# A decoder trunk on Trainium2: the classical sum of up leaves its bank earlier, p2 is multiplied second, and a layer's first feed-forward block has classical pairs only

## The chip, the cores and the metric

The kernel runs on one core of a Trainium2 chip, as one program with one launch. Its time is the device time in microseconds; the median of three runs counts. A core has TensorE (matrix products, into the banks of PSUM), VectorE and ScalarE (elementwise work, both read PSUM), GpSimd, and SyncE, which issues most DMA transfers from HBM. Each engine works through its own list of instructions in order and waits on semaphores of the others.

## The reference, cut to what matters

256 tokens of width 2048 pass through two layers. Each has a token-mixing part (differential attention, a gated recurrence, gated linear attention) and then the feed-forward part, where the change lies:

```python
for l in range(DEPTH):                       # 2 layers
    h = rms_norm(x, pre_mix_norm[l])
    ...                                      # 12 + 4 blocks of products, mixers
    h = rms_norm(x, pre_ffn_norm[l])
    hid = silu(einsum('bsd,df->bsf', h, w_ffn_gate[l])) * einsum('bsd,df->bsf', h, w_ffn_up[l])
    ff = einsum('bsf,fd->bsd', hid, w_ffn_down[l])
    x = x + rms_norm(ff, post_ffn_norm[l])
```

All is float32; the width of hid is 5632 = 11 x 512.

## The kernel before, in words

**Products.** An operand is kept as two float32r parts, hi + lo. Each product of 128 x 128 activations by 128 x 512 weights is three matmuls into one PSUM accumulator of 128 x 512 (hi.hi, hi.lo, lo.hi; `multiply`, L433, matmuls at L437 to L439; in `block`, L402 to L404). 256 tokens are two halves, t = 0 and 1. Weights come by DMA in pieces of 512 KB (two chunks of 128 x 512, tile `raw`, five buffers). `split` (L337) makes the parts of a chunk: ScalarE casts hi (tile `hilo`, ten buffers), VectorE subtracts to get lo. `feed` (L366) runs splits ahead of the products, at most ten of them, for a split needs a `hilo` buffer that an earlier product has left. All ScalarE and VectorE instructions are issued at L180, a helper, so they are told apart by their tiles.

**The feed-forward part.** hid is made in 11 blocks of 512 columns, f = 0 to 10, gate and up together (`gate_up`, `pair_block`, L442). The products with the down weights stand between them, as `ffn_order` (L56) says: after f = 0 none, after f = 1 to 8 two blocks, after f = 9 four, after f = 10 the last four. A down block has four chunks for each f that its part holds: part 0 is f = 0 alone, so the four down blocks after f = 1 and f = 2 have four chunks each; most others have eight.

**C and S pairs.** A block takes the 16 chunks of the contraction two at a time, eight pairs. A C pair is classical: 2 matrices x 2 chunks x 2 halves = 8 products, 24 matmuls. An S pair gets the same with seven products, 21 matmuls, by a Strassen-like scheme. It multiplies sums of weight chunks (t1 to t4, made by VectorE, then split like the rest) and sums of activations (the "forms", made once per layer by `make_forms`). The order of pairs is "CSCSCSCS", for f = 1 "CCSCSCSS". The classical sums and some of the seven products share accumulators: x (up, second half of the tokens), p2, q4 and q3 lie in the four banks of tag `acc`, as do the two accumulators of each down block; p1, q5 and p6 with p7 lie in others (tags `tr`, `o`, `sc`). In the profile gu_p stands for p1, p2, p6 and p7, and gu_q for q3, q4 and q5.

**Working a block off.** `evac` is called after each product of the last S pair, in the order of PRODUCTS (L104). ScalarE copies p1 to m1; VectorE then makes, with eight additions, u2 and u3 (tile u) and c11, c12, c21, c22 (tiles c_c). x is read by one of these: c22 + x, after q4. A job, `hidden`, later applies silu and the product with up, turns the rows with TensorE (tile tpu) and splits them into hid.

**The first block.** f = 0 starts while the normalised activations are still arriving, chunk by chunk. Its order is 12 single chunks of gate, six of up, an S pair, six of up, an S pair (FIRST_ORDER, L53): two S pairs. `make_forms` is called in one go after the 12 chunks of gate: one addition of 128 x 2048, four of 128 x 512, and four splits, in the queues of VectorE and ScalarE at that place.

**Order.** The order of instructions is the program's. Side work (norms, `hidden`, scales) is written as jobs that a small planner (`Lane`) runs between products, by a clock that it estimates itself; `lane.require` runs jobs until something is done.

Of the kernel before, what the change touches and what calls it, by code (L numbers as in the profile page):

```python
# [19 lines left out]
P = 128  # L20
S = 256
# [26 lines left out]

# [3 lines left out]
FIRST_C = 6  # L52
FIRST_ORDER = "G" * 2 * FIRST_C + "UUUUUUSUUUUUUS"  # L53

# [13 lines left out]
def pair_order(f):  # L68


    order = []
    if f == 0:
        at = {"G": 0, "U": 0, "S": FIRST_C}
        for kind in FIRST_ORDER:
            order += quad(at[kind]) if kind == "S" else [("GU".index(kind), at[kind])]
            at[kind] += 1
        return order
    at = {"C": 0, "S": N_C}
    for kind in SECOND_PAIRS if f == 1 else PAIRS:
        p = at[kind]  # L80
        at[kind] += 1
        order += quad(p) if kind == "S" else [(m, k) for m in range(2) for k in (2 * p, 2 * p + 1)]
    return order
# [19 lines left out]
QUAD = ("b11", "t1", "t2", "t3", "t4", "b21", "b22")  # L103
PRODUCTS = ("p1", "q5", "p6", "p7", "q4", "p2", "q3")  # L104
# [95 lines left out]
def tile_hybrid_trunk(ctx, tc, x, xT, w_in, w_out, w_gu, w_down, post_norms, lams,  # L200
# [74 lines left out]
    for l in range(DEPTH):  # L275
        for n0, n in IN_ORDER:
            plain(w_in[l][:, n0:n0 + n], DC)
        cols = [slice(b * 512, (b + 1) * 512) for b in range(4)]
        for c in cols:
            plain(w_out[l][:, c], DC)  # L280
        for kind, f, b in ffn_order():
            if kind == "down":
                f0, f1 = FFN_PARTS[f]
                plain(w_down[l][f0 * 512:f1 * 512, cols[b]], 4 * (f1 - f0))
                continue
            recipes, i = [], 0
            for kind in FIRST_ORDER if f == 0 else SECOND_PAIRS if f == 1 else PAIRS:
                k = 1 if kind in "GU" else 4
                recipes += [(name, i) for name in QUAD] if kind == "S" else [("raw", i + j) for j in range(k)]
                i += k  # L290
            add_block([w_gu[l, f, i] for i in range(DC)], recipes)
# [3 lines left out]
    for b, (n, count) in enumerate(blocks):  # L295
        b %= per_layer
        w = b in (0, 14, 15, 16, per_layer - 2, per_layer - 1) and len(wider) > 0
        wider += [w and i % 8 in (1, 4, 6) and (b != 16 or i < 2 * FIRST_C) for i in range(count)]

    read_by, left = [], Counter()  # L300
    for b, kind, i in items:
        for c in {"raw": (i,), "b11": (i + 1,), "t2": (i,), "b21": (i + 2,), "b22": (i + 3,)}.get(kind, ()):
            left[c // 2] += 1
    full_at = 0
    for b, kind, i in items:
        for c in {"raw": (i,), "b11": (i + 1,), "t2": (i,), "b21": (i + 2,), "b22": (i + 3,)}.get(kind, ()):
            left[c // 2] -= 1
        while full_at in left and left[full_at] == 0:
            full_at += 1
        read_by.append(full_at)  # L310
# [26 lines left out]
    def split():  # L337
# [7 lines left out]
        if kind == "b11":  # L345
            up1, gate1, up2 = raw_chunk(i), raw_chunk(i + 1), raw_chunk(i + 3)
            dve.free = max(dve.free, raws[(i + 3) // 2][1])
            summed("t1", gate1, up1)
            summed("t2", sums["t1"], up2)
# [7 lines left out]
        if kind == "t2":  # L357
            summed("t3", raw_chunk(i), raw_chunk(i + 3))
            summed("t4", sums["t2"], raw_chunk(i + 2))
# [82 lines left out]
    def pair_block(f, ah, al, forms, hidden_before, evac):  # L442
# [11 lines left out]
        acc = {k: pp.tile([P, 512], F32, tag="acc", name=f"gu_{k}", bufs=4) for k in ("x", "q4", "p2", "q3")}  # L454
# [11 lines left out]
        last_c = 2 * (FIRST_C if f == 0 else N_C)  # L466

        def classic(j, m, c, t):
            k = sums_of[m][t]
            n_c[k] += 1  # L470
            multiply(acc[k], parted(c, t), j, begin(k), k == "x" and n_c[k] == last_c)
            lane.tick()

        def seven(j, p, final):
            if "p1" not in acc:
                lane.require(*hidden_before)
                acc["p1"] = pp.tile([P, 512], F32, tag="tr", name="gu_p1", bufs=1)
                acc["q5"] = pp.tile([P, 512], F32, tag="o", name="gu_q5", bufs=1)
                sc = pp.tile([P, 2, 512], F32, tag="sc", name="gu_p67", bufs=1)
                acc["p6"], acc["p7"] = sc[:, 0, :], sc[:, 1, :]  # L480
# [14 lines left out]
        if f == 0:  # L495
            at = [0, 0]
            while min(at) < last_c:
                able = [t for t in range(NT) if at[t] < last_c and (t == 1 or at[0] - at[1] < AHEAD)
                        and done.get(("h", t, at[t]), math.inf) <= lane.clk]
                if not able:  # L500
                    lane.idle()
                    continue
                t = min(able, key=lambda t: at[t])
                feed(j + at[t] + 1)
                classic(j + at[t], 0, at[t], t)
                at[t] += 1
                used[0] = j + min(at)
                if ("h", 1, 7) not in done:
                    feed(j + at[0] + LOOK_F, used[0])
                else:  # L510
                    feed(used[0] + LOOK_W, used[0])
            j += last_c
            forms.extend(make_forms(ah, al))
            at = {"U": 0, "S": FIRST_C - N_C}
            for kind in FIRST_ORDER[last_c:]:
                p = at[kind]
                at[kind] += 1
                if kind == "S":
                    seven(j, p, p == N_S - 1)
                    j += 7  # L520
                    continue
                feed(j + 1)
                for t in range(NT):
                    classic(j, 1, p, t)
                j += 1
                used[0] = j
                feed(j + LOOK_W, j)
            return
# [229 lines left out]
    for l in range(DEPTH):  # L758
# [530 lines left out]
        def make_forms(ah, al):  # L1289

            full = mw[:, 0, :].rearrange("p (c t) -> p c t", t=S)[:, :2 * N_S, :]
            lane.require(*(("h", 1, c) for c in range(DC)))
            dve.tensor_tensor(out=full, in0=ah[:, 2 * N_C:, :].bitcast(F32), in1=al[:, 2 * N_C:, :].bitcast(F32),
                              op=ALU.add)
# [3 lines left out]
            dve.tensor_tensor(out=s1, in0=a21, in1=a22, op=ALU.subtract)  # L1298
            dve.tensor_tensor(out=s3, in0=a11, in1=a21, op=ALU.subtract)
            dve.tensor_tensor(out=s2_, in0=s1, in1=a11, op=ALU.subtract)  # L1300
            dve.tensor_tensor(out=s4_, in0=a12, in1=s2_, op=ALU.add)
            made = []
            for q in range(N_S):
                form = pm.tile([P, 4, 2, P], F32R, tag="s4", name="form", bufs=NS4)
                act.free = max(act.free, dve.free)
                split_scaled(form[:, :, 0, :], form[:, :, 1, :], s[:, q], None)
                made.append(form)
            return made
# [6 lines left out]

        def gate_up(f):
            if f == 0 or f % 2:
                hid.append(pm.tile([P, 2, 2, 4, S], F32R, tag="big", name="hid", bufs=5))
            got = {}

            def evac(k, acc):
# [3 lines left out]

                if k == "p1":
# [3 lines left out]
                    for names in (("c11", "c21"), ("c12", "c22")):  # L1330
                        pair = pm.tile([P, 2, 512], F32, tag="s4", name="_".join(names), bufs=NS4)
                        got[names[0]], got[names[1]] = pair[:, 0, :], pair[:, 1, :]
                    act.copy(got["m1"], acc["p1"])
                if k == "p7":
                    dve.free = max(dve.free, act.free)
# [3 lines left out]

                    add("c22", acc["q5"], got["u3"], ALU.subtract)  # L1340
                if k == "q4":
                    add("c22", got["c22"], acc["x"])
                    add("c21", got["u3"], acc["q4"])
                if k == "p2":
                    add("c11", got["m1"], acc["p2"])
                    add("c12", acc["q5"], got["u2"], ALU.subtract)
                    lane.free["tr"] = lane.free["o"] = dve.free + W_DROP
                if k == "q3":
# [3 lines left out]
            def hidden():  # L1352
# [7 lines left out]
                for t in range(NT):  # L1360
                    tag = "tr" if t == 0 else "o"
                    yield dve.through(0.25, tag) if t == 0 else (0.0, tag, None)
                    tp = turned(got[names[t][0]], tag, name="tpu")
                    ts = slice(t * P, (t + 1) * P)
                    split_scaled(hid_at(f, 0)[:, :, ts], hid_at(f, 1)[:, :, ts], tp, None)
                    dve.drops(tag)
                done[l, "hid", f] = True

            pair_block(f, hh, hl, forms, [(l, "hid", f - 1)] if f else [], evac)
# [25 lines left out]
        for kind, i, b in ffn_order():  # L1395
            if kind == "gu":
                gate_up(i)
# [14 lines left out]
W_HID = 1.0  # L1412

# [53 lines left out]
```

## Time and profile before

| | |
|---|---|
| median of 3 runs | 2328.54 us (2325.47 to 2328.74) |
| the profiled execution | 2328.21 us, its span 2326.5 us |
| mean granted TensorE clock | 0.982 |
| TensorE, VectorE, ScalarE busy | 96%, 79%, 58% of the span |
| matmuls | 10152 |
| HBM read | 412.85 MB |

A row of the timeline has start, duration (both us), engine, line, operation, the tiles written and read, their shapes, a count, and in brackets how long the engine had stood idle before it and who ended that. A row of the stretches has its limits and length, then for TensorE, its weight loads, VectorE, ScalarE and GpSimd the busy us with the number of instructions, then the granted TensorE clock (1.00 is full speed), the DMA share and GB/s. A matmul's duration is longer than the distance to the next one, since they are pipelined.

### The profile page before, as it was taken

To read this page: it belongs to the slowest core of one execution; us is meant where nothing else is said; L and a number is where in the kernel's file an instruction comes from. 1 tells how busy PE (TensorE), PEld (TensorE's weight loads), DVE (VectorE), ACT (ScalarE), POOL (GpSimd) and SP (SyncE) were. 2 spreads that over 40 slices of the span, in tenths; PEclk is the share of its full clock that TensorE was granted. 3 is DMA by queue.
4 is the path that set the end of the run, shared out by engine and by line. 5 is a ranking of instruction groups with operands and counts; after the bars stand their busy time and mean duration, and the time that the engine had idled before them with its cause. 6 is when DMAs were issued, how large, how long until landed. Compare 5 with 4: busy or idle time off the path is not lost. (4 is left out here: it accounts for less than half of the span.)

```text
span 2326.5 us, 30575 instructions
## 1 busy us (share of the span) xinstructions
PE 2231.5 (96%) x10152; PEld 1813.8 (78%) x10152; DVE 1842.1 (79%) x3335; ACT 1343.2 (58%) x2633; POOL 13.3 (1%) x33
## 2 busy tenths in 40 slices
PE   8999999899999999999999999998999999999998
PEld 6777878777777877777877788886777777877776
DVE  6766866988888888888686677579988888888885
ACT  6446755666555555555564466566665555555553
POOL 0000000000000000000000000000000000000000
PEclk9999999999999999999999999999999999999999
DMA  8553654455555555565655536554555555555563
GB/s 282 168 163 97 217 177 172 160 175 183 191 190 188 173 182 182 187 199 187 207 159 153 159 109 207 175 176 162 178 191 184 196 190 187 175 181 181 185 200 140
DMA packets 175070, 416.95 MB, mean 179 GB/s; under 512 B 13344, under 2 KB 24128, under 8 KB 174912
## 3 DMA queue, kind: packets, MB, share of 16 engines
q1 hardware_dynamic: 173056, 409.75, 53.5%
q0 software_dynamic: 1280, 4.20, 0.7%
q8 instruction: 80, 1.31, 0.2%
q10 hardware_dynamic: 576, 1.05, 0.1%
q14 instruction: 78, 0.64, 0.1%
HBM read 412.85 MB, written 2.10 MB: 178 GB/s over the span
## 5 line engine op out<-in xcount | busy, mean ns | idle before, releaser
L180 DVE TENSOR_TENSOR hilo<-raw,hilo 128x512 fp32r<-128x512 f32 (+1 forms) x1484 | 964.0, 677 | 341.2 <-ACT hilo L180 333.2
L180 ACT CAST hilo<-raw 128x512 fp32r<-128x512 f32 (+1 forms) x1484 | 859.6, 612 | 356.9 <-PE down L404 117.2
L402 PE MATMUL down<-hilo,hid 128*128 128x512 f32 x704 | 290.4, 413 | 60.2 <-DVE c_c L180 60.2
L180 ACT CAST hilo<-t 128x512 fp32r<-128x512 f32 x336 | 207.4, 621 | 192.9 <-DVE t L180 108.1
L402 PE MATMUL in<-hilo,hh 128*128 128x512 f32 (+1 forms) x768 | 301.1, 392 | 5.8 <-ACT hilo L180 5.8
L403 PE MATMUL in<-hilo,hh 128*128 128x512 f32 (+1 forms) x768 | 287.2, 374 | 1.6 <-DVE hilo L180 1.6
L404 PE MATMUL in<-hilo,hl 128*128 128x512 f32 (+1 forms) x768 | 287.6, 375 | 0.8 <-DVE hl L180 0.8
L404 PE MATMUL down<-hilo,hid 128*128 128x512 f32 x704 | 286.5, 407 | 0.0
L403 PE MATMUL down<-hilo,hid 128*128 128x512 f32 x704 | 285.7, 406 | 0.0
L180 DVE TENSOR_TENSOR hilo<-t,hilo 128x512 fp32r<-128x512 f32 x336 | 219.5, 686 | 13.6 <-ACT hilo L180 12.2
L402 PEld LDWEIGHTS down<-hilo,hid 128*128 128x128 f32 x704 | 138.9, 197 | 96.9 <-issue 68.0
L437 PE MATMUL gu_q<-hilo,hh 128*128 128x512 f32 x452 | 177.1, 392 | 0.1
L439 PE MATMUL gu_q<-hilo,hl 128*128 128x512 f32 x452 | 176.6, 391 | 0.1
L438 PE MATMUL gu_q<-hilo,hh 128*128 128x512 f32 x452 | 176.4, 390 | 0.0
L402 PEld LDWEIGHTS in<-hilo,hh 128*128 128x128 f32 x768 | 145.3, 189 | 30.7 <-ACT hilo L180 6.3
L404 PEld LDWEIGHTS in<-hilo,hl 128*128 128x128 f32 x768 | 144.8, 188 | 27.7 <-DVE hl L180 1.3
L403 PEld LDWEIGHTS in<-hilo,hh 128*128 128x128 f32 x768 | 145.4, 189 | 23.8 <-DVE hilo L180 3.2
L404 PEld LDWEIGHTS down<-hilo,hid 128*128 128x128 f32 x704 | 139.2, 198 | 31.5 <-DVE hid L180 0.5
L403 PEld LDWEIGHTS down<-hilo,hid 128*128 128x128 f32 x704 | 140.1, 199 | 29.6
L437 PE MATMUL gu_p<-hilo,hh 128*128 128x512 f32 x352 | 138.2, 393 | 8.6 <-DVE c_c L180 5.9
L439 PE MATMUL gu_p<-hilo,hl 128*128 128x512 f32 x352 | 137.5, 391 | 0.0
L438 PE MATMUL gu_p<-hilo,hh 128*128 128x512 f32 x352 | 137.4, 390 | 0.0
(221 smaller groups left out, 3236.8 us busy)
## 6 DMA issues: line engine op xcount, KB each, us to landing
raw<-in_w_gu_dram SPq DMA_DIRECT2D x352, 512.0 KB, 3.3
raw<-in_w_down_dram SPq DMA_DIRECT2D x176, 512.0 KB, 4.5
raw<-in_w_in_dram SPq DMA_DIRECT2D x159, 512.0 KB, 4.2
raw<-in_w_out_dram SPq DMA_DIRECT2D x64, 512.0 KB, 4.6
raw<-in_w_in_dram SPq DMA_DIRECT2D x32, 264.0 KB, 2.9
gain<-in_post_norms_dram POOLq DMA_DIRECT2D x16, 256.0 KB, 3.9
x<-in_x_dram SPq DMA_DIRECT2D x8, 256.0 KB, 7.5
xt<-in_xT_dram SPq DMA_DIRECT2D x7, 256.0 KB, 7.2
```

The source lines that it names most:

```text
L180: return getattr(self.engine, name)(*args, **kwargs)
L402: nc.tensor.matmul(acc[t], ah, hi, start=(i == 0), stop=False)
L403: nc.tensor.matmul(acc[t], ah, lo, start=False, stop=False)
L404: nc.tensor.matmul(acc[t], al, hi, start=False, stop=(i == last))
L437: nc.tensor.matmul(acc, a[0], hi, start=start, stop=False)
L438: nc.tensor.matmul(acc, a[0], lo, start=False, stop=False)
L439: nc.tensor.matmul(acc, a[1], hi, start=False, stop=stop)
```

## The change

Three things are edited.

1. When the last classical product of a block is in x, ScalarE copies x into c22 at once. PRODUCTS puts p2 second, and its addition c11 = m1 + p2 follows it. q5 is added to c22 when it is there, and u3 is subtracted later; c12 moves ahead of q4. VectorE still has eight additions, ScalarE has one copy more.
2. The parts of an S pair come in another order: b21 follows b11, and each of the sums t1 to t4 is made one part ahead of its use, where before they were made two at a time.
3. f = 0 becomes two plain blocks, gate and then up, of 16 classical chunks each (192 matmuls in place of 186). The gate's accumulators are worked off by ScalarE's silu, those of up by one VectorE operation each. `make_forms` becomes a job of twelve steps, 1.36 us of the planner's clock apart, that starts when gate is done. Forms are needed first in f = 1.

```diff
-FIRST_C = 6
-FIRST_ORDER = "G" * 2 * FIRST_C + "UUUUUUSUUUUUUS"
...
-QUAD = ("b11", "t1", "t2", "t3", "t4", "b21", "b22")
-PRODUCTS = ("p1", "q5", "p6", "p7", "q4", "p2", "q3")
+QUAD = ("b11", "b21", "t1", "t2", "t3", "t4", "b22")
+PRODUCTS = ("p1", "p2", "q5", "p6", "p7", "q4", "q3")
...
         if kind == "b11":
-            up1, gate1, up2 = raw_chunk(i), raw_chunk(i + 1), raw_chunk(i + 3)
-            dve.free = max(dve.free, raws[(i + 3) // 2][1])
-            summed("t1", gate1, up1)
-            summed("t2", sums["t1"], up2)
+            summed("t1", raw_chunk(i + 1), raw_chunk(i))
+        if kind == "b21":
+            summed("t2", sums["t1"], raw_chunk(i + 3))
+        if kind == "t1":
+            summed("t3", raw_chunk(i), raw_chunk(i + 3))
+        if kind == "t2":
+            summed("t4", sums["t2"], raw_chunk(i + 2))
...
         act.copy(hi, r)
-        if kind == "t2":
-            summed("t3", raw_chunk(i), raw_chunk(i + 3))
-            summed("t4", sums["t2"], raw_chunk(i + 2))
...
-        acc = {k: pp.tile([P, 512], F32, tag="acc", name=f"gu_{k}", bufs=4) for k in ("x", "q4", "p2", "q3")}
+        acc = {k: pp.tile([P, 512], F32, tag="acc", name=f"gu_{k}", bufs=4) for k in ("x", "p2", "q4", "q3")}
...
         def classic(j, m, c, t):
             k = sums_of[m][t]
             n_c[k] += 1
-            multiply(acc[k], parted(c, t), j, begin(k), k == "x" and n_c[k] == last_c)
+            final = k == "x" and n_c[k] == 2 * N_C
+            multiply(acc[k], parted(c, t), j, begin(k), final)
+            if final:
+                evac(k, acc)
             lane.tick()
...
+            for o, a, b, op in ((s1, a21, a22, ALU.subtract), (s3, a11, a21, ALU.subtract),
+                                (s2_, s1, a11, ALU.subtract), (s4_, a12, s2_, ALU.add)):
+                dve.tensor_tensor(out=o, in0=a, in1=b, op=op)
+                yield after(W_FORM)
             for q in range(N_S):
                 form = pm.tile([P, 4, 2, P], F32R, tag="s4", name="form", bufs=NS4)
-                act.free = max(act.free, dve.free)
                 split_scaled(form[:, :, 0, :], form[:, :, 1, :], s[:, q], None)
-                made.append(form)
-            return made
+                forms.append(form)
+                yield after(W_FORM)
+            done[l, "forms"] = True
+
+        lane.add(2, make_forms(hh, hl, mw))
...
+        def gate_up_first():
+            sg = [None, None]
+            def gate(t, acc):
+                if t == 0:
+                    scale_known()
+                sg[t] = wide("sg", "e")
+                act.activation(sg[t], acc, AF.Silu, scale=s2f[t])
+            def up(t, acc):
+                dve.scalar_tensor_tensor(out=sg[t], in0=acc, scalar=s2f[t], in1=sg[t],
+                                         op0=ALU.mult, op1=ALU.mult)
+                if t == 1:
+                    lane.add(0, turn_hidden(0, sg))
+            hid.append(pm.tile([P, 2, 2, 4, S], F32R, tag="big", name="hid", bufs=5))
+            block(halves(hh, hl), "gate", gate, fresh=True)
+            done[l, "gate"] = True
+            block(halves(hh, hl), "up", up)
...
+                if k == "x":
+                    for names in (("c12", "c22"), ("c11", "c21")):
+                        pair = pm.tile([P, 2, 512], F32, tag="s4", name="_".join(names), bufs=NS4)
+                        got[names[0]], got[names[1]] = pair[:, 0, :], pair[:, 1, :]
+                    act.copy(got["c22"], acc["x"])
                 if k == "p1":
                     scale_known()
                     got["m1"] = wide("m1", "on")
                     got["u2"], got["u3"] = wide("u2", "e"), wide("u3", "e")
...
                     act.copy(got["m1"], acc["p1"])
+                if k == "p2":
+                    dve.free = max(dve.free, act.free)
+                    add("c11", got["m1"], acc["p2"])
+                if k == "q5":
+                    add("c22", got["c22"], acc["q5"])
                 if k == "p7":
-                    dve.free = max(dve.free, act.free)
                     add("u2", got["m1"], acc["p6"])
                     add("u3", got["u2"], acc["p7"])
                     lane.free["sc"] = dve.free + W_DROP
-
-                    add("c22", acc["q5"], got["u3"], ALU.subtract)
-                if k == "q4":
-                    add("c22", got["c22"], acc["x"])
-                    add("c21", got["u3"], acc["q4"])
-                if k == "p2":
-                    add("c11", got["m1"], acc["p2"])
                     add("c12", acc["q5"], got["u2"], ALU.subtract)
                     lane.free["tr"] = lane.free["o"] = dve.free + W_DROP
+                    add("c22", got["c22"], got["u3"], ALU.subtract)
+                if k == "q4":
+                    add("c21", got["u3"], acc["q4"])
                 if k == "q3":
                     add("c12", got["c12"], acc["q3"])
                     lane.add(0, hidden())
...
-            pair_block(f, hh, hl, forms, [(l, "hid", f - 1)] if f else [], evac)
+            pair_block(f, hh, hl, forms, [(l, "hid", f - 1), (l, "forms")], evac)
```

More of the change, by code (lines that the diff above doesn't have):

```diff
@@ L68, in pair_order @@
 def pair_order(f):
+    if f == 0:
+        return [(m, k) for m in range(2) for k in range(DC)]
     order = []
[L72 to L77, printed above, removed]
     at = {"C": 0, "S": N_C}
@@ L286, in tile_hybrid_trunk @@
             recipes, i = [], 0
[L287 to L291, printed above, removed]
+            srcs = [w_gu[l, f, i] for i in range(DC)]
+            if f == 0:
+                for half in (srcs[:DC // 2], srcs[DC // 2:]):
+                    add_block(half, [("raw", i) for i in range(DC)])
+                continue
+            for kind in SECOND_PAIRS if f == 1 else PAIRS:
+                recipes += [(name, i) for name in QUAD] if kind == "S" else [("raw", i + j) for j in range(4)]
+                i += 4
+            add_block(srcs, recipes)
     per_layer = len(blocks) // DEPTH
@@ L297, in tile_hybrid_trunk @@
         w = b in (0, 14, 15, 16, per_layer - 2, per_layer - 1) and len(wider) > 0
-        wider += [w and i % 8 in (1, 4, 6) and (b != 16 or i < 2 * FIRST_C) for i in range(count)]
+        wider += [w and i % 8 in (1, 4, 6) for i in range(count)]
     read_by, left = [], Counter()
     for b, kind, i in items:
-        for c in {"raw": (i,), "b11": (i + 1,), "t2": (i,), "b21": (i + 2,), "b22": (i + 3,)}.get(kind, ()):
+        for c in {"raw": (i,), "b11": (i + 1,), "t1": (i,), "t2": (i + 2,), "b22": (i + 3,)}.get(kind, ()):
             left[c // 2] += 1
@@ L305, in tile_hybrid_trunk @@
     for b, kind, i in items:
-        for c in {"raw": (i,), "b11": (i + 1,), "t2": (i,), "b21": (i + 2,), "b22": (i + 3,)}.get(kind, ()):
+        for c in {"raw": (i,), "b11": (i + 1,), "t1": (i,), "t2": (i + 2,), "b22": (i + 3,)}.get(kind, ()):
             left[c // 2] -= 1
@@ L440, in multiply, with pair_block @@
         lane.clk += 3 * (512 / 2400 + 0.0025)
-    def pair_block(f, ah, al, forms, hidden_before, evac):
+    def pair_block(f, ah, al, forms, before, evac):
         base = starts[turn[0]]
@@ L465, in pair_block @@
         parted = halves(ah, al)
-        last_c = 2 * (FIRST_C if f == 0 else N_C)
         def classic(j, m, c, t):
@@ L475, in seven @@
             if "p1" not in acc:
-                lane.require(*hidden_before)
+                lane.require(*before)
                 acc["p1"] = pp.tile([P, 512], F32, tag="tr", name="gu_p1", bufs=1)
@@ L494, in pair_block @@
         j = base
[L495 to L528, printed above, removed]
         at = {"C": 0, "S": 0}
@@ L1287, in tile_hybrid_trunk, with make_forms @@
         forms = []
-        def make_forms(ah, al):
+        def make_forms(ah, al, mw):
+            yield 0.0, None, lane.has((l, "gate"), *(("h", 1, c) for c in range(DC)))
             full = mw[:, 0, :].rearrange("p (c t) -> p c t", t=S)[:, :2 * N_S, :]
-            lane.require(*(("h", 1, c) for c in range(DC)))
-            dve.tensor_tensor(out=full, in0=ah[:, 2 * N_C:, :].bitcast(F32), in1=al[:, 2 * N_C:, :].bitcast(F32),
-                              op=ALU.add)
+            for c in range(0, 2 * N_S, 2):
+                k = slice(2 * N_C + c, 2 * N_C + c + 2)
+                dve.tensor_tensor(out=full[:, c:c + 2, :], in0=ah[:, k, :].bitcast(F32), in1=al[:, k, :].bitcast(F32),
+                                  op=ALU.add)
+                yield after(W_FORM)
             a11, a21, a12, a22 = (full[:, i::2, t * P:(t + 1) * P] for i in range(2) for t in range(NT))
@@ L1297, in make_forms @@
             s1, s2_, s3, s4_ = (s[:, :, i, :] for i in range(4))
[L1298 to L1302, printed above, removed]
+            for o, a, b, op in ((s1, a21, a22, ALU.subtract), (s3, a11, a21, ALU.subtract),
+                                (s2_, s1, a11, ALU.subtract), (s4_, a12, s2_, ALU.add)):
+                dve.tensor_tensor(out=o, in0=a, in1=b, op=op)
+                yield after(W_FORM)
             for q in range(N_S):
                 form = pm.tile([P, 4, 2, P], F32R, tag="s4", name="form", bufs=NS4)
-                act.free = max(act.free, dve.free)
                 split_scaled(form[:, :, 0, :], form[:, :, 1, :], s[:, q], None)
-                made.append(form)
-            return made
+                forms.append(form)
+                yield after(W_FORM)
+            done[l, "forms"] = True
+        lane.add(2, make_forms(hh, hl, mw))
         hid = []
@@ L1314, in hid_at, with turn_hidden @@
             return hid[(f + 1) // 2][:, part, (f + 1) % 2]
+        def gate_up_first():
[14 more added lines that the diff above has]
+            block(halves(hh, hl), "up", up)
+        def turn_hidden(f, sg):
+            for t in range(NT):
+                tag = "tr" if t == 0 else "o"
+                yield dve.through(0.25, tag) if t == 0 else (0.0, tag, None)
+                tp = turned(sg[t], tag, name="tpu")
+                ts = slice(t * P, (t + 1) * P)
+                split_scaled(hid_at(f, 0)[:, :, ts], hid_at(f, 1)[:, :, ts], tp, None)
+                dve.drops(tag)
+            done[l, "hid", f] = True
         def gate_up(f):
-            if f == 0 or f % 2:
+            if f % 2:
                 hid.append(pm.tile([P, 2, 2, 4, S], F32R, tag="big", name="hid", bufs=5))
@@ L1329, in evac @@
                     got["u2"], got["u3"] = wide("u2", "e"), wide("u3", "e")
-                    for names in (("c11", "c21"), ("c12", "c22")):
-                        pair = pm.tile([P, 2, 512], F32, tag="s4", name="_".join(names), bufs=NS4)
-                        got[names[0]], got[names[1]] = pair[:, 0, :], pair[:, 1, :]
                     act.copy(got["m1"], acc["p1"])
+                if k == "p2":
[3 more added lines that the diff above has]
+                    add("c22", got["c22"], acc["q5"])
                 if k == "p7":
-                    dve.free = max(dve.free, act.free)
                     add("u2", got["m1"], acc["p6"])
@@ L1359, in hidden @@
                                              op0=ALU.mult, op1=ALU.mult)
[L1360 to L1367, printed above, removed]
-            pair_block(f, hh, hl, forms, [(l, "hid", f - 1)] if f else [], evac)
+                yield from turn_hidden(f, (got["c11"], got["c21"]))
+            pair_block(f, hh, hl, forms, [(l, "hid", f - 1), (l, "forms")], evac)
         def down(part, b):
@@ L1396, in tile_hybrid_trunk @@
             if kind == "gu":
-                gate_up(i)
+                gate_up(i) if i else gate_up_first()
             else:
@@ L1412 @@
 W_HID = 1.0
+W_FORM = 1.36
 def kernel(**inputs):
```

## The prediction

> **What bounds the kernel now.** I read the page's shares first, then the waits of TensorE, then the timeline where the longest wait recurs.
>
> ```profile
> span 2326.5 us, 30575 instructions
> ...
> PE 2231.5 (96%) x10152; PEld 1813.8 (78%) x10152; DVE 1842.1 (79%) x3335; ACT 1343.2 (58%) x2633; POOL 13.3 (1%) x33
> ```
>
> TensorE is busy 96% of the span, so the time is its matmuls plus what it waits, plus any stretch in which it runs slowly. No other engine is near full over the whole span. The waits of TensorE (total us, times, longest):
>
> ```profile
> PE down L402 <- DVE c_c L180: 60.2, 20, 3.5
> PE gu_q L437 <- ACT form L180: 7.0, 2, 3.5
> PE gu_p L437 <- DVE c_c L180: 5.9, 2, 3.0
> ...
> PE gu_p L437 <- DVE hid L180: 2.7, 2, 1.5
> ```
>
> The first row is the case: 20 times, once after each gate-up block that a down block follows (f = 1 to 10, two layers), the down block's first matmul waits 3.0 us for VectorE to work the products off. The other rows belong to a layer's first block (f = 0). Here is one of the 20, the end of f = 2 in the first layer; first TensorE:
>
> ```profile
> 551.36 0.39 PE L437 MATMUL gu_p<-hilo,hh 128*128 128x512 f32 x1
> ...
> 555.67 0.39 PE L438 MATMUL gu_q<-hilo,form 128*128 128x512 f32 x1
> 555.89 0.39 PE L439 MATMUL gu_q<-hilo,form 128*128 128x512 f32 x1
> 559.23 0.47 PE L402 MATMUL down<-hilo,hid 128*128 128x512 f32 x1 [2.95 <-DVE c_c L180]
> ...
> 560.00 0.54 PE L402 MATMUL down<-hilo,hid 128*128 128x512 f32 x1
> ...
> 563.33 0.49 PE L404 MATMUL down<-hilo,hid 128*128 128x512 f32 x1
> ```
>
> At 551.36 the last pair's seven products (21 matmuls) begin; the last starts at 555.89, so 20 steps take 4.53: 0.2265 us a matmul. The next could start at 556.12 and starts at 559.23: 3.11 lost, the 2.95 of the wait and 0.16 in which the pipe drains. Then comes a second loss: from 560.00 to 563.33 eight steps take 3.33 instead of 1.81, and 559.23 to 560.00 holds three steps in 0.77 instead of 0.68. **Each wait drags some 1.6 us of slow matmuls behind it.** VectorE and ScalarE in the same stretch:
>
> ```profile
> 553.95 1.90 DVE L180 TENSOR_TENSOR hilo<-raw,hilo 128x512 fp32r<-128x512 f32 x3 [0.31 <-ACT hilo L180]
> 555.77 0.68 DVE L180 TENSOR_TENSOR u<-m,gu_p 128x512 f32<-128x512 f32 x1
> ...
> 558.41 0.68 DVE L180 TENSOR_TENSOR c_c<-c_c,gu_x 128x512 f32<-128x512 f32 x1
> ...
> 560.20 0.68 DVE L180 TENSOR_TENSOR c_c<-m,gu_p 128x512 f32<-128x512 f32 x1
> 560.80 0.69 DVE L180 TENSOR_TENSOR c_c<-gu_q,u 128x512 f32<-128x512 f32 x1
> 561.40 0.69 DVE L180 TENSOR_TENSOR hilo<-raw,hilo 128x512 fp32r<-128x512 f32 x1
> 562.00 0.69 DVE L180 TENSOR_TENSOR c_c<-c_c,gu_q 128x512 f32<-128x512 f32 x1
> ```
>
> ```profile
> 550.26 0.62 ACT L180 CAST hilo<-raw 128x512 fp32r<-128x512 f32 x1 [0.75 <-PE gu_x L439]
> 551.61 1.31 ACT L180 CAST hilo<-raw 128x512 fp32r<-128x512 f32 x2 [0.73 <-PE gu_x L439]
> 552.82 0.58 ACT L180 COPY m<-gu_p 128x512 f32<-128x512 f32 x1
> 553.30 3.64 ACT L180 CAST hilo<-raw 128x512 fp32r<-128x512 f32 x6
> ```
>
> VectorE starts one operation every 0.60 us (560.20, 560.80, 561.40) and is never idle here. The operation that reads x ends at 558.41 + 0.68 = 559.09, and 0.14 later the down block starts: it had been waiting for x's bank, though x's sum was complete at 551.36. Which bank a new accumulator takes is seen at the end of f = 0:
>
> ```profile
> 451.85 0.77 PE L437 MATMUL gu_p<-hilo,hh 128*128 128x512 f32 x1 [2.96 <-DVE c_c L180]
> ```
>
> ```profile
> 451.02 0.68 DVE L180 TENSOR_TENSOR c_c<-c_c,gu_x 128x512 f32<-128x512 f32 x1
> ...
> 454.15 0.68 DVE L180 TENSOR_TENSOR c_c<-m,gu_p 128x512 f32<-128x512 f32 x1
> ```
>
> Block 1's first product goes to its p2. It starts when block 0's x has been read (451.70), long before block 0's p2 has (454.15). So the next block takes the banks in the order in which they come free.
>
> **The change, part by part.** (1) *x and p2.* ScalarE copies x at the start of the last S pair, so the first bank is free at about 551.36 + 0.16 + 0.6 = 552.1, 4 us before the down block asks. Its second half asks three matmuls later, at 556.12 + 0.68 = 556.80, for the bank freed second, now p2's. When is c11 = m1 + p2 done? p2 itself ends at 551.36 + 6 x 0.2265 + 0.16 = 552.9; VectorE's queue decides. u2 started at 555.77. In the new order p7 is the fifth product, so one more split and two more additions (c11, c22 + q5) stand before u2: 555.77 + 3 x 0.60 = 557.6. c11 stands five operations before u2, hence 554.6, ending 555.3. If ScalarE's extra copy delays the casts by its whole 0.5 (m's row: 0.58), c11 ends at 555.8. With the 0.14 that is 0.9 to 1.4 us in time. So all 20 waits go: 60.2 + 20 x 0.16 + 20 x 1.6 = **95.4 us**.
>
> The copies themselves, 20 x 0.6 us, lie on ScalarE, and what is queued behind them are casts that at 550.26 and 551.61 wait for the same gu_x matmuls anyway. VectorE's operations per block stay at eight; they only move. Without that cover a copy would cost its 0.6 each, 12 us.
>
> What is late next: the banks of q4 and q3. c21 comes five operations after u2 and, as u2, u3 and c12 hang on each other, some 0.2 later: it ends near 557.6 + 3.2 + 0.7 = 561.5, with the copy's delay 562.0; c12's second addition 1.2 later. The second down block takes these banks. In part 0 (after f = 1 and 2) a down block has four chunks, 24 matmuls, so the second begins at 556.12 + 5.44 = 561.56 and loses between 0.6 and 1.1 in all; elsewhere eight chunks or more put it at 567 or later and nothing is lost. Four such places: **+3 us**, bounds 0 and 8.
>
> (2) *The order of the splits* (b21 second, sums one by one instead of two by two): same number of operations and of transfers. I take 0: none of TensorE's waits above names a split in a gate-up block, so an evener queue has nothing to win; the bound upwards is one VectorE step, 0.6, in every tenth of 80 pairs, 5 us.
>
> (3) *First block.* Two S pairs of 42 matmuls become two C pairs of 48: 6 more a layer, 12 x 0.2265 = **+2.7**. The four waits below the first row go, because the forms are made piecemeal during the up block, block 0 has one operation a half to work off, and its hidden rows are turned without the eight additions: 7.0 + 5.9 + 2.7 + 6 x 0.16 = 16.6. The slow matmuls after them I read from the granted clock of these stretches:
>
> ```profile
> 398.00:448.50 50.50, 46.84 (x207) 37.83 (x206) 46.40 (x98) 34.71 (x83) 0.00 (x0) 0.97 0.44 143
> 448.50:490.00 41.50, 37.06 (x155) 29.98 (x154) 36.32 (x59) 22.55 (x37) 0.00 (x0) 0.92 0.47 159
> 490.00:1140.00 650.00, 619.93 (x2692) 508.91 (x2691) 555.62 (x879) 377.41 (x639) 1.61 (x3) 0.97 0.56 188
> ...
> 1556.00:1648.00 92.00, 83.42 (x369) 67.20 (x368) 84.45 (x159) 58.36 (x122) 0.00 (x0) 0.98 0.46 152
> ```
>
> 0.03 x 50.5 + 0.08 x 41.5 + 0.02 x 92 = 6.7 us. So 16.6 + 6.7 = **23.3 us** go. The forms cost VectorE and ScalarE what they did, in twelve steps beside an up block of 96 x 0.2265 = 21.7 us; with 16 splits that is 28 x 0.60 = 17 us of VectorE in it, so they are covered. Uncovered, they come back.
>
> The third row above (ten blocks) also checks part 1: 3% of 650 is 19.5 us of lost clock in one layer, 16 by my 1.6 a wait. It shows too that VectorE has room: 555.6 us busy, and 650 - 47.7 = 602 would be left.
>
> **Sum:** 2326.5 - 95.4 - 23.3 + 2.7 + 3 = 2213.5 us of span. The profiled run took 2328.21, 1.7 over its span, and lies 0.3 under the median of 2328.54: **2215 us**, 4.9% less.
>
> [...]
>
> **Rivals.** *The slow stretch is not the wait's.* If something else lowers the clock near block ends, the 32 + 6.7 us stay: 2254. [...] Against: the slow steps follow the waits and stand nowhere else in these rows. 3%. [...]
>
> *c11 comes late.* If VectorE runs 2.5 us later than at f = 2 (f = 1 ends on two S pairs running, and the removed wait was also its time to catch up; or casts queue behind the copy), the second half waits 1 us, 20 times: 2235, more with clock loss. Against: the ring holds ten splits ahead, and 40 us of room a layer. 10%.
>
> *The first block gives nothing:* forms and scale become late elsewhere, its 23.3 us stay: 2238. For: VectorE is busy 46.4 of the 50.5 us from 398 on. Against: the up block's room worked out above. 6%.
>
> *Slower: the early bank is not the one that down takes.* Were banks dealt in a fixed turn, so that down begins in q4's, it would wait for c21, 561.5 to 562.0 + 0.14, from 556.12: 5.4 to 6.0 instead of 3.1, some 2.6 x 20 = 52 us more, less 20.6 from block 0: 2360. It decides from the point where c21 ends after 559.1. For: p2 and q4 change places in the list of accumulators, which would matter only in a fixed turn. Against: the start at 451.85. 4%; another 1% for no change.
>
> **How the numbers follow.** The forecast keeps 76%, within 2204 (no residue, clock loss by the windows) and 2228 (residue and all copies uncovered). Up to 2240 the range takes in the rivals of the late c11 and of the first block as priced; what lies beyond (clock, bank, no change, a worse c11) and below 2204 is some 14%: range 2204 to 2240. A change of 0.2%, 4.7 us, is about what can be told from none here. Faster: the forecast and the three partial rivals, 95%, less 2% for what I have not seen: 93%; of these 2% and the 1% for no change, 2% go to the same time and 1% joins the bank rival's 4%: slower 5%.
>
> **What would show it.** Right: the row of down waiting for c_c is gone or under 5 us, the granted clock reads 0.99 to 1.00 from 490 on, an x copy stands on ScalarE some 4 us before each first down matmul, and the only rest is in down blocks after f = 1 and 2. The forms row is gone and block 1 starts about 444. Wrong: a wait of down for c_c or ScalarE of over 1 us in most blocks (c11 late, or the wrong bank), half clock without a wait, or new waits of gu matmuls for hilo (VectorE out of room).

## The result and the profile after

The changed kernel takes 2215.04 us (median of 4 runs, 2214.26 to 2215.51) against 2327.92 for the kernel before (4 runs): a ratio of 0.9516, 95% interval 0.950 to 0.9533. Forecast were 2215 us and a range of 2204 to 2240. Shown first are lines of the page, then the whole of what TensorE waited for. Line numbers have moved: L399 to L401 are the matmuls of plain blocks, L434 to L436 those of pair blocks, L173 the helper of VectorE and ScalarE.

```profile
span 2212.5 us, 30519 instructions
...
PE 2193.5 (99%) x10164; PEld 1792.4 (81%) x10164; DVE 1798.9 (81%) x3297; ACT 1335.8 (60%) x2639; POOL 13.3 (1%) x33
```

```profile
PE in L399 <- ACT hilo L173: 5.5, 1, 5.5
PE down L399 <- DVE c_c L173: 1.7, 8, 0.3
PE in L401 <- DVE hl L173: 0.8, 1, 0.8
PE tpx L556 <- DVE hl L173: 0.6, 1, 0.6
PE down L399 <- ACT hid L173: 0.5, 2, 0.2
PE in L400 <- DVE hilo L173: 0.3, 1, 0.3
```

The 60.2 us of down on c_c have become 1.7, in eight places; the waits for the forms, of block 1 for c_c and for the bank in which hid's rows are turned are gone. What is left, 9.4 us, is mostly the kernel's start. All of TensorE's waits together came to 85.6 us before, so 76.2 went. The mean granted clock rose from 0.982 to 0.998: (1 - 0.982) x 2326.5 = 41.9 us of clock lost before, 4.4 now, 37.5 less; what is left lies in the last 8.5 us, after the last matmul, where the clock reads 0.58. With 12 more matmuls, 2.7, and some 24 pipe drains of 0.16 less, 3.8, that makes 114.8; the spans differ by 114.0.

The same block end as in the prediction, f = 2 of the first layer, in the timeline of TensorE:

```profile
532.81 0.39 PE L434 MATMUL gu_p<-hilo,hh 128*128 128x512 f32 x1
...
537.34 0.39 PE L436 MATMUL gu_q<-hilo,form 128*128 128x512 f32 x1
537.57 0.39 PE L399 MATMUL down<-hilo,hid 128*128 128x512 f32 x1
...
538.25 0.39 PE L399 MATMUL down<-hilo,hid 128*128 128x512 f32 x1
...
543.23 0.47 PE L399 MATMUL down<-hilo,hid 128*128 128x512 f32 x1
...
544.34 0.50 PE L399 MATMUL down<-hilo,hid 128*128 128x512 f32 x1 [0.17 <-DVE c_c L173]
```

of VectorE:

```profile
536.28 0.68 DVE L173 TENSOR_TENSOR c_c<-m,gu_p 128x512 f32<-128x512 f32 x1
...
539.28 0.68 DVE L173 TENSOR_TENSOR u<-m,gu_p 128x512 f32<-128x512 f32 x1
...
542.40 0.68 DVE L173 TENSOR_TENSOR c_c<-u,gu_q 128x512 f32<-128x512 f32 x1
543.00 0.69 DVE L173 TENSOR_TENSOR hilo<-raw,hilo 128x512 fp32r<-128x512 f32 x1
543.60 0.68 DVE L173 TENSOR_TENSOR c_c<-c_c,gu_q 128x512 f32<-128x512 f32 x1
```

and of ScalarE:

```profile
533.01 0.59 ACT L173 COPY c_c<-gu_x 128x512 f32<-128x512 f32 x1 [0.68 <-PE gu_x L436]
533.49 1.14 ACT L173 CAST hilo<-raw 128x512 fp32r<-128x512 f32 x2
534.53 0.59 ACT L173 COPY m<-gu_p 128x512 f32<-128x512 f32 x1
```

The first down matmul follows the last q3 by 0.23, without a gap. The copy of x ended 4 us earlier (533.60). c11 ends at 536.96; the down block's second half asks at 538.25, so there were 1.15 us to spare after the 0.14 of a handover. The second down block starts at 543.23 in place of 543.01, and its second half waits until c12 has its last addition (544.28). VectorE begins u2 6.5 us after the last pair began.

The stretches that the prediction used (the third ends at 1090, since the part is shorter now; columns as there):

```profile
398.00:448.50 50.50, 50.47 (x235) 41.69 (x234) 43.45 (x92) 36.11 (x81) 0.00 (x0) 1.00 0.52 171
448.50:490.00 41.50, 41.17 (x182) 33.82 (x182) 38.67 (x64) 26.54 (x46) 0.00 (x0) 1.00 0.59 198
490.00:1090.00 600.00, 599.10 (x2675) 495.03 (x2675) 537.00 (x864) 370.18 (x637) 1.61 (x3) 1.00 0.61 202
```

TensorE is busy 599.1 of 600 us at full clock.

### The profile page after: what moved, and what is told of

Its sections match the earlier page's. It is cut to its first block, busy times and chain, and to the rows that moved or that the text cites. A ratio compares the mean times of both kernels' runs of the same rounds, so it can differ in the third digit from the quotient of the medians.

```text
span 2212.5 us, 30519 instructions
## 1 busy us (share of the span) xinstructions
PE 2193.5 (99%) x10164; PEld 1792.4 (81%) x10164; DVE 1798.9 (81%) x3297; ACT 1335.8 (60%) x2639; POOL 13.3 (1%) x33
## 4 chain that ended last, share of the span: by engine, by line
PE 92%; DVE 5%; DMA 1%; ACT 1%; issue 1%; SPq 0%; DVEq 0%; ACTq 0%
PE in L399 7%; PE down L399 7%; PE in L401 7%; PE down L401 7%; PE in L400 7%; PE down L400 7%; PE gu_q L434 5%; PE gu_q L436 5%; PE gu_q L435 5%; PE gu_p L436 5%; PE gu_p L434 5%; PE gu_p L435 5%; PE op L399 3%; PE op L401 3%; PE op L400 3%; DVE hilo L173 2%
## 5 line engine op out<-in xcount | busy, mean ns | idle before, releaser
L173 DVE TENSOR_TENSOR hilo<-raw,hilo 128x512 fp32r<-128x512 f32 (+1 forms) x1488 | 965.6, 676 | 281.9 <-ACT hilo L173 273.6
L173 ACT CAST hilo<-raw 128x512 fp32r<-128x512 f32 (+1 forms) x1488 | 858.0, 614 | 274.8 <-PE gu_x L436 94.2
L399 PE MATMUL in<-hilo,hh 128*128 128x512 f32 (+1 forms) x768 | 301.4, 392 | 5.5 <-ACT hilo L173 5.5
L173 ACT CAST hilo<-t 128x512 fp32r<-128x512 f32 x320 | 198.8, 622 | 170.8 <-DVE t L173 119.8
L401 PE MATMUL in<-hilo,hl 128*128 128x512 f32 (+1 forms) x768 | 287.9, 375 | 0.8 <-DVE hl L173 0.8
L399 PE MATMUL down<-hilo,hid 128*128 128x512 f32 x704 | 277.1, 394 | 2.4 <-DVE c_c L173 1.7
L401 PE MATMUL down<-hilo,hid 128*128 128x512 f32 x704 | 274.7, 390 | 0.0
L400 PE MATMUL down<-hilo,hid 128*128 128x512 f32 x704 | 274.3, 390 | 0.0
L173 DVE TENSOR_TENSOR hilo<-t,hilo 128x512 fp32r<-128x512 f32 x320 | 208.4, 686 | 8.3 <-ACT hilo L173 8.0
L399 PEld LDWEIGHTS in<-hilo,hh 128*128 128x128 f32 x768 | 145.5, 189 | 30.0 <-ACT hilo L173 5.5
L401 PEld LDWEIGHTS in<-hilo,hl 128*128 128x128 f32 x768 | 144.9, 189 | 27.6 <-DVE hl L173 1.3
L399 PEld LDWEIGHTS down<-hilo,hid 128*128 128x128 f32 x704 | 132.2, 188 | 34.1 <-DVE c_c L173 3.7
L434 PE MATMUL gu_q<-hilo,hh 128*128 128x512 f32 x400 | 156.0, 390 | 0.0
L436 PE MATMUL gu_q<-hilo,hl 128*128 128x512 f32 x400 | 155.8, 390 | 0.0
L435 PE MATMUL gu_q<-hilo,hh 128*128 128x512 f32 x400 | 155.8, 389 | 0.0
L401 PEld LDWEIGHTS down<-hilo,hid 128*128 128x128 f32 x704 | 132.2, 188 | 28.5 <-DVE hid L173 0.9
L400 PEld LDWEIGHTS down<-hilo,hid 128*128 128x128 f32 x704 | 132.3, 188 | 26.5
L434 PE MATMUL gu_p<-hilo,hh 128*128 128x512 f32 x320 | 125.0, 390 | 0.0
L436 PE MATMUL gu_p<-hilo,hl 128*128 128x512 f32 x320 | 124.6, 390 | 0.0
L435 PE MATMUL gu_p<-hilo,hh 128*128 128x512 f32 x320 | 124.6, 389 | 0.0
```

What stands on the lines that cost most here:

```text
L173: return getattr(self.engine, name)(*args, **kwargs)
L399: nc.tensor.matmul(acc[t], ah, hi, start=(i == 0), stop=False)
L400: nc.tensor.matmul(acc[t], ah, lo, start=False, stop=False)
L401: nc.tensor.matmul(acc[t], al, hi, start=False, stop=(i == last))
L434: nc.tensor.matmul(acc, a[0], hi, start=start, stop=False)
L435: nc.tensor.matmul(acc, a[0], lo, start=False, stop=False)
```

## The experiments

My theory was: the 95 us lie in the order in which banks come free against the order in which they are asked for, the slow matmuls belong to those waits, and the first block is worth 21 us by itself.

**Each edit alone.** e1 is the kernel before with the first edit; e2 has the third alone.

```diff
 e1, against the kernel before
-PRODUCTS = ("p1", "q5", "p6", "p7", "q4", "p2", "q3")
+PRODUCTS = ("p1", "p2", "q5", "p6", "p7", "q4", "q3")
 and the changed kernel's evac, with evac("x") at the end of the classical products
```

> The kernel before with the first edit alone: ScalarE copies x, p2 comes second; old order of splits, old first block with its two S pairs. My theory (the bank of x is all that the down blocks wait for, and the slow clock is the wait's): the 20 waits go, 95.4 us, with 3 left in the second down blocks of part 0; block 0 ends in the same way, so the wait of block 1 for c_c goes too with its slow matmuls, 5.9 + 0.3 + 3.3. The waits for the forms (7.0) and for hid (2.7) stay. Sum 2328 - 95.4 + 3 - 9.5 = 2226 us. Rival (the clock falls near block ends whatever is waited for): 2226 + 32 = 2258. Rival (VectorE without the new order of splits is too late for p2's bank): 1 us more in each of 20 places, 2246.

> The kernel before with the third edit alone: gate and up as two classical blocks, the forms made piecemeal beside up; x, p2 and the splits as before. My theory: 23.3 us of waits and slow matmuls go, 2.7 of matmuls come: 2328 - 20.6 = 2307 us, and the 20 waits of down for c_c stay at 60 us. Rival (the first block only gains together with the first edit): 2328 + 3 = 2331.

In e1, and in e3 and e5 below, the products of an S pair multiply other parts of the weights than they should. Each product takes the part that stands at its own place in the list, and only one of the two lists was turned; instructions, sizes and waits are those of the right pairing, the sums are not. So the change's first two edits are one. e11 is e1 with both lists turned.

```diff
 e11, against e1
-QUAD = ("b11", "t1", "t2", "t3", "t4", "b21", "b22")
+QUAD = ("b11", "b21", "t1", "t2", "t3", "t4", "b22")
 and each sum made one part ahead, as in the change
```

> The kernel before with the first two edits, which belong together (the products take the parts of an S pair in the order in which these come): copy of x, p2 second, new order of parts; the old first block stays. In e1, block 1's fifth product, q3, waited 4.1 us for the bank that came free third, read by c21, where before its first had waited 3.0 for the first bank. My theory now: that shift is the old first block's own and stays, so 2238 us, with the waits for the forms (7.0 before) and a gu_q wait of 8 us in all. Rival (the odd pairing of parts in e1 made it, not the block): 2226 us as I worked out for e1.

Measured: e1 2238.35 us, e11 2240.10, e2 2304.88 (before, in their runs, 2326.7 to 2326.9). e2 is 21.9 us faster than before; 20.6 were worked out. In e11 the down waits are at 1.7 as in the changed kernel, and 86.8 us are gained, not the 102 that I had worked out for e1. What e1 missed was block 1. Its waits, in TensorE's timeline and VectorE's:

```profile
453.50 0.76 PE L437 MATMUL gu_q<-hilo,hh 128*128 128x512 f32 x1 [4.11 <-DVE c_c L180]
```

```profile
452.68 0.68 DVE L180 TENSOR_TENSOR c_c<-u,gu_q 128x512 f32<-128x512 f32 x1
```

and in e11 the list of waits has

```profile
PE gu_q L437 <- DVE c_c L180: 6.8, 2, 3.4
...
PE gu_q L437 <- ACT form L180: 5.6, 2, 2.9
PE gu_p L437 <- DVE hid L180: 2.4, 2, 1.2
```

Block 1 follows block 0 at once and asks for four banks within 3.4 us, not for two. Its fifth product, q3, takes the third bank, q4's, and c21 ends at 453.36. With the old first block the edit only moves the wait from the first bank to the third. The rival, that the odd pairing made this wait, falls with e11. It takes the third edit to remove this wait, and that does so with the old order of products as well. Counted in TensorE's waits the parts add up: of the 85.6 us before, 59.2 are gone in e11 and 16.9 in e2, together 76.2 in the changed kernel. In time the two alone give 86.8 + 21.9 = 108.7, together 112.9; these 4 us are no more than the 95% intervals of e11 and e2 (some 4 us to either side each) leave open.

**The order of the parts alone.** e3 is the changed kernel with the old QUAD and the old places of the sums.

> The changed kernel with the old order of an S pair's splits and sums (t1 and t2 made together with b11, t3 and t4 with t2; b21 sixth). My theory: the order costs and gains nothing, 2215 us. Rival (the evener queue is what lets c11 be in time): down blocks wait up to 1 us each, up to 2235.

2214.67 us: no difference to 2215.04. The evener queue is worth nothing here; the order is there so that p2 finds its part.

**Which bank.** e4 leaves the copy out, e5 and e12 put p2 back to the sixth place (e12 with its part, so that the sums are right), e6 only turns the list in which the accumulators are made.

```diff
 e4, against the changed kernel
-                    act.copy(got["c22"], acc["x"])
-                if k == "q5":
-                    add("c22", got["c22"], acc["q5"])
...
-                    add("c22", got["c22"], got["u3"], ALU.subtract)
+                    add("c22", acc["q5"], got["u3"], ALU.subtract)
...
                 if k == "q4":
+                    add("c22", got["c22"], acc["x"])
 e5, against the changed kernel (e12: QUAD and the sums too)
-PRODUCTS = ("p1", "p2", "q5", "p6", "p7", "q4", "q3")
+PRODUCTS = ("p1", "q5", "p6", "p7", "q4", "p2", "q3")
 e6, against the changed kernel
-        acc = {... for k in ("x", "p2", "q4", "q3")}
+        acc = {... for k in ("x", "q4", "p2", "q3")}
```

> The changed kernel without the copy: VectorE adds x into c22 after q4, as it did before; p2 stays second. My theory (banks go out in the order in which they come free): p2's bank is now free first and takes the down block's first half in time; the second half takes x's, read near 9.8 us after the last pair's start and asked for at 5.4: 4.4 us of wait and some 1.6 of slow matmuls in 20 places, 2215 + 120 = 2335 us. Rival (banks in a fixed turn): the first half waits for x, 5.1 us: 2350. Rival (p2's place alone is what matters): 2215.

> The changed kernel with p2 back in the sixth place of the seven products; x is still copied early. My theory: the first half of each down block starts in time in x's bank, the second waits for the bank that is free second, now q4's, whose reader c21 ends near 9.1 us after the last pair's start; asked for at 5.4: 3.7 us and 1.6 of slow matmuls in 20 places, 2215 + 105 = 2320 us. Rival (x's bank alone is enough): 2215.

> The changed kernel with p2 and b21 both back in the sixth place and the old order of parts; x is still copied early by ScalarE, and the new first block stays. My theory, as for e5: the down block's second half waits for the bank that comes free second, q4's, 3.5 us and slow matmuls in 20 places: 2322 us. Rival (x's copy alone is enough, and e5's wait came from its odd pairing): 2215 us.

> The changed kernel with the four accumulators listed in their old order (x, q4, p2, q3); nothing else changes. My theory (the bank that is free first goes to the accumulator written first, whatever the list): no change, 2215 us. Rival (banks in a fixed turn by the list): the second half of each down block waits for q4's, 4.8 us in 20 places and slow matmuls: 2340.

Measured: e4 2331.94 us, e5 2323.19, e12 2322.69, e6 2214.57. Against the kernel before, e4 is slower by 0.22% (ratio 1.0022, 1.0012 to 1.0033) and e12 faster by 0.16% (0.9984, 0.9974 to 0.9993). **Either half of the edit alone gives back all or nearly all of the gain**, the first block's 22 us included. Against e2 (2304.88 us), which has the new first block and neither half, either half alone is slower, by 17.8 us (e12) and 27.1 us (e4). The waits of e2, e12 and e4 in turn:

```profile
PE down L399 <- DVE c_c L173: 60.4, 20, 3.5
PE down L399 <- DVE c_c L173: 71.1, 20, 3.8
PE down L399 <- DVE c_c L173: 78.4, 20, 4.4
```

The down block starts early and then waits longer, for the second bank. The end of f = 2 in e12, TensorE and then VectorE:

```profile
542.62 0.39 PE L401 MATMUL down<-hilo,hid 128*128 128x512 f32 x1
546.54 0.79 PE L399 MATMUL down<-hilo,hid 128*128 128x512 f32 x1 [3.53 <-DVE c_c L173]
```

```profile
545.80 0.68 DVE L173 TENSOR_TENSOR c_c<-u,gu_q 128x512 f32<-128x512 f32 x1
```

The first half's three matmuls run in x's bank; then the second half waits for c21 (ends 546.48), the reader of q4. In e4 the roles change, again TensorE and VectorE:

```profile
545.05 0.39 PE L401 MATMUL down<-hilo,hid 128*128 128x512 f32 x1
549.29 0.50 PE L399 MATMUL down<-hilo,hid 128*128 128x512 f32 x1 [3.85 <-DVE c_c L173]
```

```profile
548.56 0.68 DVE L173 TENSOR_TENSOR c_c<-c_c,gu_x 128x512 f32<-128x512 f32 x1
```

Now the first half is in p2's bank and the second waits for the reader of x (ends 549.24). In e6 the list is turned and nothing happens. Banks go out as they come free; the rival of a fixed turn, which had the only slower outcome, falls.

**What the copy costs.** e7 has VectorE make it, e10 issues it twice.

```diff
-                    act.copy(got["c22"], acc["x"])
+                    dve.tensor_copy(got["c22"], acc["x"])
 (e10: the line act.copy(...) twice)
```

> The changed kernel with VectorE in place of ScalarE making the copy of x. My theory: what counts is that x is read early; VectorE gets one operation of 0.6 us more ahead of c11, which had 0.9 to 1.2 us to spare, so nothing is waited for in most places, and the second down blocks of part 0 lose 0.6 more in four places: 2217 us. Rival (VectorE has no room for it): 0.6 to 1 us in each of 20 places, 2230 to 2235.

> The changed kernel with ScalarE's copy of x issued twice (the second writes the same values again). My theory: the copy is covered, since the casts behind it wait for the same matmuls and c11 has 0.9 to 1.4 us to spare: 2215 us, at most 2 more in the second down blocks of part 0. Rival (the copies are paid for): 20 x 0.6 = 12 us more, 2227.

Measured: e7 2214.79 us, the same as the changed kernel; its eight waits for c_c grow from 1.7 to 2.9 us. That the copy is ScalarE's is not what matters; that it is early is. e10 takes 2220.17, 5.1 more; neither 0 to 2 nor 12 had been right. Its waits:

```profile
PE down L399 <- DVE c_c L173: 4.9, 12, 0.7
PE down L401 <- DVE hid L173: 1.9, 2, 1.1
PE down L399 <- ACT hid L173: 1.0, 2, 0.7
```

A second copy delays the casts, and so VectorE (at f = 2 c11 begins 0.6 us later against the down block's start), where the chain is tight already: in the second down blocks of part 0 (eight of the twelve waits), in the second down block after f = 9 (four), and after f = 10, whose hid is needed eight chunks later. Some 5 of the added 12 us of ScalarE come through.

**How long a wait costs clock.** e8 and e9 issue the addition c11 five and nine times, to hold p2's bank longer.

```diff
-                    add("c11", got["m1"], acc["p2"])
+                    for _ in range(5):    # e9: 9
+                        add("c11", got["m1"], acc["p2"])
```

> The changed kernel with the addition c11 issued five times in place of once (the same values), so that p2's bank comes free 2.4 us later. My theory: 1.15 us of slack is used up, the second half of each down block waits 1.25 us, 20 x (1.25 + 0.16) = 28; the second down blocks of part 0 lose 2.4 more in four places, 10: 2253 us, with the clock at full speed if a wait of that length doesn't lower it. Rival (any wait at a block's end lowers the clock): 32 us more, 2285.

> The changed kernel with the addition c11 issued nine times, so that p2's bank comes free 4.8 us later. My theory: a wait of 3.65 us in 20 places, as long as before the change, so the slow matmuls come back with it, 20 x (3.65 + 0.16 + 1.6) = 108, and part 0's second down blocks lose 4.8 more in four places, 19: 2342 us. Rival (the slow clock had another cause, which the change took away): 32 less, 2310.

Measured: 2265.71 and 2352.91 us. The waits of e8, then its down waits between 480 and 1060 us alone, and that stretch's row:

```profile
PE down L399 <- DVE c_c L173: 38.3, 32, 1.8
...
PE down L401 <- DVE hid L173: 3.2, 2, 1.6
PE gu_p L434 <- DVE hid L173: 1.9, 2, 1.0
```

```profile
PE down L399 <- DVE c_c L173: 19.2, 16, 1.8
```

```profile
480.00:1060.00 580.00, 559.87 (x2487) 458.99 (x2485) 534.39 (x857) 349.84 (x598) 0.00 (x0) 1.00 0.59 192
```

and of e9:

```profile
PE down L399 <- DVE c_c L173: 88.5, 22, 4.7
```

```profile
470.00:1105.00 635.00, 589.01 (x2529) 482.92 (x2528) 574.22 (x914) 358.33 (x609) 0.00 (x0) 0.96 0.54 178
```

Between 480 and 1060 e8 waits for c_c 16 times, 1.2 us on average and up to 1.8, and the clock reads 1.00: these waits cost themselves and the drain. e9 waits up to 4.7 and loses 0.04 x 635 = 25 us of clock in that layer. So the slow matmuls come back with the long wait alone, with the rest of the change in place; the rival that they had another cause falls. Both runs are 11 to 13 us above what I expected. In e8 the waits for c_c grew by 36.6 us, where I had 35. Not counted were hid, late after f = 10 and in a following block (3.2 + 1.9), the drains of the other dozen waits (2), and a little clock outside that stretch: its mean is 0.997 against 0.998, 2.4 us. In e9 the waits for c_c grew by 86.8 us, where I had 92; what is over there is the clock. By its mean of 0.976, 56.4 us were lost against 4.4, so 52 where I had 32: 2.4 us for each of its 22 waits, more than the 1.6 each that I had carried over from waits of 3 us.

## Why the prediction was right

- **Bound and place.** Right: TensorE's matmuls and the 20 waits. The span fell by 114.0, the sum said 113.0.
- **x and p2, 95.4 us.** Right. Waits of down went from 60.2 to 2.2, and the clock to 1.00. The two margins worked out from VectorE's 0.60 us step were: c11 in time by 0.9 to 1.4 us (measured 1.15 at f = 2), u2 at 6.2 to 6.7 us after the last pair's start (6.5).
- **The residue, +3.** Right in size, two places short. The two halves of the second down block begin 0.92 us late in all after f = 1 (489.84 for 489.35, then 490.95 for 490.52) and 0.65 after f = 2 (543.23 for 543.01, then 544.34 for 543.91), where 0.6 to 1.1 had been worked out: 3.1 in the four places. But the places are six, not four. `FFN_PARTS` has f = 7 as a part by itself, so the down blocks after f = 9 have four chunks as well, where the prediction had "elsewhere eight chunks or more", and the second loses 0.65 there too (977.41 for 977.19, then 978.52 for 978.09). Hid after f = 10 adds 0.5. The row's 1.7 us in eight waits (six in part 0, two after f = 9) leave out the drains and the late starts that are too short for a wait to be listed.
- **Clock, 32 + 6.7 us.** Measured 37.5. e9 shows that it belongs to the waits. The 1.6 us of slow matmuls behind each wait were read at one of the 20; they follow 19 of them, and the last section sets a place with them beside the one without.
- **The order of the parts as an edit of its own: wrong in kind, right in price.** It cannot be undone alone, as p2 must find b21 second. Its price of 0 is e3's, a run that times the old order with the wrong pairing.
- **The copies.** "Without that cover a copy would cost its 0.6 each, 12 us" was not tested as such; doubled, 5.1 of 12 us come through, so the cover is thinner than the prediction made it.
- **First block, 23.3 less 2.7.** Right: e2 alone gains 21.9 us. The forms cost no wait. Block 1 begins at 442.2, 444 was said. That with the old first block the first edit would have left block 1 waiting, for the third bank (6.8 us in e11), was not in the prediction; since the third edit removes that wait, its sum came out all the same. Its "four waits below the first row" are six, two in each of three rows, and the sum has six drains for them.
- **Rivals.** c11 late falls with the waits of the changed kernel, the fixed turn of banks with e4, e6 and e12, the clock without wait with e9, the first block giving nothing with e2.

## What to carry to other kernels

Compare the order in which accumulator banks come free with the order in which the next block asks for them, bank by bank; a sum that is complete early but read late holds a bank for nothing, and one early reader without the second (e4, e12) was worse here than none (e2). Count how many banks the next consumer asks for and how fast: two at a down block, four at a pair block. And price a wait of TensorE with its aftermath: here a wait of 3 us cost 4.7 in 19 of 20 places.

## What the runs showed of the hardware

Single waits of up to 1.8 us (e8) left the clock at 1.00 over 580 us; waits of about 3 us and more (2.95 in the kernel before, 3.53 in e12) brought steps of 0.43 us in place of 0.2265 after them, but not each of them did. Of the 22 waits of down and of block 1 for c_c in the kernel before, two did not, both in the second layer: that of block 1 and that of the down block after f = 2. In its trace the clock falls 22 times before the last matmul, 21 times for 3.41 us and once, at 450.9, for twice that, so I cut the trace into stretches of this length that begin and end with the falls. Here is the kernel before at the end of f = 2, two stretches of the first layer and three of the second:

```profile
556.69:560.11 3.42, 0.88 (x4) 0.78 (x5) 3.38 (x6) 0.25 (x1) 0.00 (x0) 1.00 0.77 214
560.11:563.52 3.41, 3.41 (x10) 2.62 (x9) 3.41 (x7) 1.86 (x3) 0.00 (x0) 0.50 0.37 135
...
1710.40:1713.81 3.41, 1.92 (x9) 1.26 (x7) 3.34 (x6) 2.46 (x5) 0.00 (x0) 1.00 0.85 259
1713.81:1717.23 3.42, 1.96 (x9) 1.64 (x10) 3.42 (x7) 0.27 (x1) 0.00 (x0) 1.00 0.78 261
1717.23:1720.64 3.41, 3.41 (x17) 2.82 (x16) 3.41 (x7) 3.01 (x6) 0.00 (x0) 1.00 0.47 154
```

Both waits are 2.95 us long. In the first layer 2.54 us of the idle time fall into one stretch, and the whole of the next one runs at 0.50, which costs 1.7 us. In the second layer the same idle time is split, 1.49 and 1.46 us, and the clock stays at 1.00. The other falls of this trace begin a whole number of 3.41 us from this one. After the first 20 us, 23 of its stretches at full clock held 1.94 us or more without a matmul, the one after the last matmul among them, and each was followed by one at 0.50; none of those at full clock with 1.51 us or less was.

In this trace, what went with a fall was not a wait's length as such (2.95 us in both places), nor what was waited for (c_c in both), but how much idle time lay in one stretch. e8 shows it from the other side, where the waits for hid of 0.37 and 1.58 us after f = 10, each shorter than the 1.8 us above, lie in one stretch with 1.96 us of idle time, and the next reads 0.50:

```profile
1070.86:1074.27 3.41, 1.45 (x8) 0.78 (x7) 3.41 (x7) 1.28 (x3) 0.00 (x0) 1.00 0.79 256
1074.27:1077.69 3.42, 3.42 (x9) 2.63 (x9) 0.99 (x2) 0.62 (x1) 0.00 (x0) 0.50 0.91 317
```

Where the stretches begin differs between these two runs (0.3 us behind a multiple of 3.41 from the span's start in the kernel before, 2.5 in e8); that it is chance which wait of 3 us escapes is my estimate from that, and no run shows it.
